# Start of a conformer/attention encoder kernel: two output pairs share the activations, squares summed in PSUM, first loads in halves on two queues, and a bias table written head by head in the weight queue

## The chip, the cores and the metric

The kernel runs on one core of a Trainium2 chip as one launch. The metric is the device time of that launch in microseconds. The kernel before takes 2254.43 us (median of 3 runs, 2253.42 to 2255.34). A core has a matrix engine (TensorE, PE in the profile; its weight loads are PEld), VectorE (DVE), ScalarE (ACT), GpSimd (POOL) and SyncE (SP), which here only issues DMAs. ACT and POOL issue DMAs as well. All engines run their own instruction streams in order and meet at semaphores.

## The reference

The input is x of shape 1 x 256 x 2048 in float32. Layer 0 is a conformer convolution module and a convolutional feed-forward network; layer 1 is differential attention and a second such network; each is added to x, with an RMS norm in front of it and one at the very end.

```
for i in range(2):
    h = rmsnorm(x, mix_norm[i])
    m = conformer_conv(h, ...) if i == 0 else diff_attention(h, ..., rel_bias, lambda_init)
    x = x + m
    x = x + conv_ffn(rmsnorm(x, ffn_norm[i]), ...)
return rmsnorm(x, final_norm_g)

conformer_conv: u = h @ w_in + b_in              # 2048 -> 4096
                a, gate = split(u);  u = a * sigmoid(gate)
                u = silu(layernorm(causal_dwconv31(u) + dw_b))
                return u @ w_out + b_out
diff_attention: 16 heads, two score maps each; bias_table[h, bucket(k - q)] is added
                to the scores and keys of later 64-chunks are masked
conv_ffn:       u = causal_dwconv3(h @ w_up);  (silu(gate) * val) @ w_down
```

## The kernel before

Everything is held transposed: channels in the 128 partitions, the 256 positions along the free axis. x is 8 tiles `X[pr]` of 128 x 2 x 256. A weight matrix is used in **pairs**: 2 x 128 output channels, for which the 16 input tiles of 128 channels are gone through in 4 **steps** of 4. Each step has its own weight tile of 128 x 1024 (512 KB). To keep float32 accuracy every operand is split into a rounded part `hi` and a remainder `lo`, and a product is three matmuls: hi by hi, hi by the activation's lo, lo by hi. A step of the module w_in is 24 such matmuls of 256 columns, a pair 96.

A weight tile comes through SP's queue into one of 5 `raw` buffers (`load_w`), ACT rounds it into one of 6 `hi` buffers and DVE or POOL subtracts to give one of 6 `lo` buffers (`split_w`; the argument `lo` of `pair` names the engine). `ahead` keeps the splits 4 steps in front of the matmuls and the loads 5 in front of the splits. An activation tile is split by one ACT and one DVE instruction (`split_act`, L279 and L280).

`setup` issues the first loads, splits 4 weight tiles and the 16 activation tiles in a hand-written order for DVE, ACT and POOL, squares x on ACT and sums the squares on DVE in SBUF (`x_square`, L326 to L333), and then computes the norm: `norm_cols` adds the halves and sums over channels with ones-matmuls (L286), raises the mean square to the power -1/2 on POOL (L298, `rc`), and `norm_rows` spreads the result over the partitions with two matmuls (L292) and copies it to `rstd`. The matmuls of w_in don't wait for the norm, since rstd is multiplied onto their result.

`conv_module` has 16 w_in pairs. After a pair, `post` multiplies the PSUM tile by rstd (L453), takes the sigmoid gate and writes `u` into a padded buffer `cpad` (L457). PSUM has two tiles `pp` for pairs, so pair 2 needs pair 0's post to be done. Then u is written to DRAM (`ud`, L469) and read back in four shifted copies (`R`, L473); POOL builds 32 x 32 diagonals `dg` from the filter (L482); `taps` runs 12 of the 31 filter taps as matmuls (L498), and DVE adds the other 19 (L536). After the first pair POOL also writes the 18 diagonals of the last pair (L489, `Y` and `A`). What is deferred by `at` runs so many steps later; elsewhere the order on an engine is set by the framework's scheduler.

`attn_setup` runs at the first step of layer 0's feed-forward network. It makes the 16 x 384 table of relative biases, writes it 128 times per head to DRAM as `d1` with one DMA from POOL (L759, 3 MB), and writes the mask into each head's part with 16 more (L766). In the attention `bias` reads a skewed 128 x 256 view of a head's part into `bm` (L851).

Of the kernel before, what the change touches and what calls it, by code (L numbers as in the profile page):

```python
# [61 lines left out]
class Builder:  # L62
# [72 lines left out]
    def load_w(self):  # L135
        i = self.np_
        self.np_ += 1
        w = self.W[i]
        w["raw"] = self.rawp.tile([P, self.c.NW], F32, tag="raw", name=self.nm("raw"))
        self.nc.sync.dma_start(w["raw"][:, :w["n"]], w["src"])  # L140

    def split_w(self):
# [7 lines left out]
        nc.scalar.copy(hi[:, :n], raw[:, :n])  # L150
        eng = nc.gpsimd if w["lo_eng"] == "g" else nc.vector
        ins = eng.tensor_tensor(lo[:, :n], raw[:, :n], hi[:, :n].bitcast(F32), ALU.subtract)  # L152
        if w["lo_eng"] == "g":
            self.pool_lo = ins.ins
        w["hi"] = hi[:, :n].rearrange("p (k c) -> p k c", c=w["cols"])
        w["lo"] = lo[:, :n].rearrange("p (k c) -> p k c", c=w["cols"])

    def ahead(self, i):

        N = len(self.W)  # L160
        while self.ns < min(N, i + 1):
# [158 lines left out]
    def x_square(self, st, pr, eng=None):  # L320
# [3 lines left out]
        if st["n"] == 0:  # L324
            st["ssq"] = self.const.tile([P, 2, S], F32, tag="ssq", name=self.nm("ssq"), bufs=1)
            nc.scalar.activation(st["ssq"], x, AF.Square)  # L326
        else:
# [4 lines left out]
            else:  # L332
                (eng or nc.gpsimd).tensor_tensor(st["ssq"], st["ssq"], sq, ALU.add)  # L333
        st["n"] += 1

    def norm_cols(self, st):
# [3 lines left out]
        self.nc.vector.tensor_tensor(f, q[:, 0, :], q[:, 1, :], ALU.add)  # L340
# [8 lines left out]
        self.rsqrt_cols(st["rc"], ps[:, 0:4:2], 1.0 / self.c.D)  # L349
# [41 lines left out]
    def setup(self, n0):  # L391
# [22 lines left out]
        with self.tc.manual_schedule(engines={ET.DVE, ET.Activation, ET.Pool}):  # L414
            for pr in range(KT // 2):
                if pr % 2 == 0 and pr // 2 < 4:
                    self.split_w()
                for j in range(2):
                    m = 2 * pr + j
                    n0["xh"][m] = self.act_tile()  # L420
                    self.split_act(n0["xh"][m][1], self.X[pr][:, j, :], self.col("mixg", m))

            for pr in range(KT // 2):
                if pr % 3 == 2:
                    self.ahead(4 + pr // 3)
                self.x_square(n0, pr, nc.vector)
        self.norm_cols(n0)
        self.norm_rows(n0)
# [6 lines left out]
        for i in range(3):  # L435
# [6 lines left out]
    def conv_module(self, nin, nout):  # L442
# [6 lines left out]
        def post(i, ps):  # L449
            with self.tc.high_priority():  # L450

                t = ps[:, :, 0:S]
                nc.vector.tensor_tensor(t, t, nin["rstd"].unsqueeze(1).to_broadcast([P, 2, S]), ALU.mult)  # L453
                sg = self.b1("G")
                nc.scalar.activation(sg, t[:, 1, :], AF.Sigmoid, bias=self.col("bin", KT + i))
                u = self.cpad[i % 3]
                nc.vector.scalar_tensor_tensor(u[:, CK - 1:CK - 1 + S], t[:, 0, :], self.col("bin", i), sg, ALU.add,  # L457
# [18 lines left out]
            queue = self.tc.issue_after(self.pool_lo) if i == 0 else ExitStack()  # L476
            with queue:
# [189 lines left out]
        for i in range(KT):  # L667
            off = self.pair(a["w_in"], off, c.kcs, lambda k: nin["xh"][k], lambda ps, i=i: post(i, ps),
# [406 lines left out]
```

## Time and profile before

| | before |
|---|---|
| median of 3 runs | 2254.43 us |
| profiled execution, its own time | 2254.46 us |
| span of its trace | 2252.7 us |
| PE busy | 2205.2 us (98%) |
| DVE busy | 1634.2 us (73%) |
| ACT busy | 1200.7 us (53%) |
| POOL busy | 273.5 us (12%) |
| DMA, mean over the span | 185 GB/s |
| mean granted TensorE clock | 0.991 |

The span runs from the first to the last instruction; the launch's own time is 1.8 us longer. A busy PE is not a PE at full pace: matmuls overlap and their ends are modelled. So stretches are compared by how many matmuls they hold, and gaps by the idle time that the timeline gives in brackets together with what ended it.

### The profile page before, as it was taken

The numbers are of one execution on the slowest core, as the hardware profiler recorded it, in microseconds if no ns is written. First come the engines' busy times: TensorE is split into PE (matmuls) and PEld (weight loads), VectorE is DVE, ScalarE is ACT, GpSimd is POOL, SyncE is SP. The second block draws the span as 40 slices with busy tenths as digits, with TensorE's granted clock in tenths as the row PEclk, the third lists the DMA queues.
The fourth block names the chain that finished last, engine by engine and source line by source line (L and its number), as shares of the span: only waits on it lengthen the run. The fifth ranks groups of instructions, "written<-read, shape, count | busy, mean of one in ns | idle before, by whom it ended". The sixth has DMA issues, their size and how long they took to land.

```text
span 2252.7 us, 34458 instructions
## 1 busy us (share of the span) xinstructions
PE 2205.2 (98%) x13238; PEld 1937.4 (86%) x13238; DVE 1634.2 (73%) x2471; ACT 1200.7 (53%) x1796; POOL 273.5 (12%) x181
## 2 busy tenths in 40 slices
PE   5999899999999999999999999999999999999998
PEld 5999788888888888888888888888888888888887
DVE  4788675877767777677777787767777677676774
ACT  4333454655545555455565665555555455554554
POOL 4788500100000000000100000100000000000002
PEclk8999999999999999999999999999999999999998
DMA  6677357866666666666655555566666666666662
GB/s 236 192 218 215 112 185 164 244 187 189 188 189 191 189 188 187 192 189 186 193 176 177 171 171 174 170 192 186 190 187 187 188 188 187 190 188 190 187 188 94
DMA packets 126004, 417.51 MB, mean 185 GB/s; under 512 B 14416, under 2 KB 26704, under 8 KB 125840
## 3 DMA queue, kind: packets, MB, share of 16 engines
q1 hardware_dynamic: 113040, 400.42, 57.2%
q10 hardware_dynamic: 11520, 11.45, 2.0%
q0 software_dynamic: 1280, 3.46, 1.3%
q8 instruction: 103, 1.69, 0.3%
q14 instruction: 61, 0.50, 0.1%
HBM read 407.55 MB, written 7.72 MB: 184 GB/s over the span
## 4 chain that ended last, share of the span: by engine, by line
PE 94%; DMA 2%; DVE 0%; issue 0%; ACT 0%; POOL 0%; ACTq 0%; POOLq 0%; DVEq 0%
PE pp L238 48%; PE pp L239 25%; PE pp L229 7%; PE pp L236 4%; PE pp L235 2%; PE pp L813 1%; PE pp L815 1%; PE pp L814 1%; DMA raw<-in_w_up_dram 1%; PE s L863 1%; PE s L498 1%; PE o L898 0%; DMA R<-ud 0%; PE t L498 0%; PE s L507 0%; DMA ud<-cpad 0%
## 5 line engine op out<-in xcount | busy, mean ns | idle before, releaser
L238 PE MATMUL pp<-act,hi 128*128 128x512 f32 x3902 | 1380.7, 396 | 5.8 <-DVE act L645 3.1
L239 PE MATMUL pp<-act,lo 128*128 128x256 f32 x3902 | 1095.7, 281 | 0.0
L150 ACT CAST hi<-raw 128x1024 fp32r<-128x1024 f32 x752 | 788.1, 1049 | 532.2 <-PE pp L238 186.2
L152 DVE TENSOR_TENSOR lo<-raw,hi 128x1024 fp32r<-128x1024 f32 x686 | 844.4, 1232 | 299.2 <-ACT hi L150 287.5
L238 PEld LDWEIGHTS pp<-act,hi 128*128 128x128 f32 x3902 | 732.5, 188 | 165.6 <-DVE act L645 3.4
L239 PEld LDWEIGHTS pp<-act,lo 128*128 128x128 f32 x3902 | 739.4, 189 | 10.2
L238 PE MATMUL pp<-actb,hi 128*128 128x512 f32 x856 | 308.5, 397 | 1.4 <-ACT hi L150 1.4
L239 PE MATMUL pp<-actb,lo 128*128 128x256 f32 x856 | 241.3, 282 | 0.8 <-DVE lo L152 0.8
L333 POOL TENSOR_TENSOR ssq<-ssq,Z 128x512 f32<-128x512 f32 x24 | 35.6, 1484 | 1518.4 <-ACT Z L329 1518.3
L229 PE MATMUL pp<-act,hi 128*128 128x256 f32 x1088 | 203.4, 289 | 9.0 <-ACT act L279 6.2
L238 PEld LDWEIGHTS pp<-actb,hi 128*128 128x128 f32 x856 | 161.3, 188 | 40.2 <-ACT hi L150 1.7
L229 PEld LDWEIGHTS pp<-act,hi 128*128 128x128 f32 x1088 | 173.7, 196 | 15.5 <-ACT act L279 6.2
L152 POOL TENSOR_TENSOR lo<-raw,hi 128x1024 fp32r<-128x1024 f32 x66 | 158.0, 2413 | 56.3 <-ACT hi L150 55.6
L239 PEld LDWEIGHTS pp<-actb,lo 128*128 128x128 f32 x856 | 162.6, 190 | 1.2 <-DVE lo L152 1.1
L266 ACT COPY E<-pp 128x512 f32<-128x512 f32 x104 | 60.9, 585 | 184.1 <-PE pp L236 184.1
L229 PE MATMUL pp<-act,lo 128*128 128x256 f32 x544 | 156.4, 288 | 2.0 <-POOL lo L152 1.5
L382 ACT COPY E<-pp 128x512 f32<-128x512 f32 x109 | 63.9, 586 | 170.7 <-PE pp L236 163.0
L268 DVE TENSOR_TENSOR E<-pp,E 128x512 f32<-128x512 f32 x104 | 71.9, 691 | 108.2 <-ACT E L266 108.2
L704 DVE SCALAR_TENSOR_TENSOR Y<-fpad,prm,Y 128x256 f32<-128x256 f32 x352 | 146.9, 478 | 0.0
L384 DVE TENSOR_TENSOR x<-pp,x 128x512 f32<-128x512 f32 x101 | 69.8, 691 | 87.8 <-ACT E L382 87.4
L701 ACT ACTIVATE Y<-fpad,prm 128x256 f32<-128x256 f32 x176 | 96.3, 595 | 48.3 <-DVE fpad L697 48.3
L229 PEld LDWEIGHTS pp<-act,lo 128*128 128x128 f32 x544 | 106.7, 196 | 2.4 <-POOL lo L152 1.7
(194 smaller groups left out, 1797.5 us busy)
## 6 DMA issues: line engine op xcount, KB each, us to landing
raw<-in_w_up_dram SPq DMA_DIRECT2D x352, 512.0 KB, 4.1
raw<-in_w_down_dram SPq DMA_DIRECT2D x176, 512.0 KB, 4.1
raw<-in_w_in_dram SPq DMA_DIRECT2D x64, 512.0 KB, 4.4
raw<-in_w_qk_dram SPq DMA_DIRECT2D x64, 512.0 KB, 3.6
raw<-in_w_out_dram SPq DMA_DIRECT2D x32, 512.0 KB, 3.8
raw<-in_w_v_dram SPq DMA_DIRECT2D x32, 512.0 KB, 3.7
raw<-in_w_o_dram SPq DMA_DIRECT2D x32, 512.0 KB, 3.8
R<-ud ACTq DMA_DIRECT2D x52, 132.0 KB, 4.8
```

What stands on the lines that cost most here:

```text
L150: nc.scalar.copy(hi[:, :n], raw[:, :n])
L152: ins = eng.tensor_tensor(lo[:, :n], raw[:, :n], hi[:, :n].bitcast(F32), ALU.subtract)
L229: nc.tensor.matmul(ps[:, 0:S], w[:, kk, cs], xt[:, x, :], start=(k == first and n == 0), stop=(k == last and n == 2))
L236: nc.tensor.matmul(*main, start=False, stop=True)
L238: nc.tensor.matmul(*main, start=(k == first), stop=False)
L239: nc.tensor.matmul(*corr, start=False, stop=False)
L266: nc.scalar.copy(cs, ps[:, :, S:])
L268: nc.vector.tensor_tensor(t, ps[:, :, 0:S], cs, ALU.add)
L382: nc.scalar.copy(cs, ps[:, :, S:])
L384: nc.vector.tensor_tensor(x, ps[:, :, 0:S], x, ALU.add)
L701: nc.scalar.activation(y[:, j, :], u[:, j, FK - 1:], AF.Identity, scale=self.col("fw", ch * FK + FK - 1), bias=self.col("fb", ch))
L704: nc.vector.scalar_tensor_tensor(y[:, j, :], u[:, j, q:q + S], self.col("fw", ch * FK + q), y[:, j, :], ALU.mult, ALU.add)
```

## The change

It has five parts. (1) The steps of w_in pairs 0 and 1 alternate, so each activation tile serves both before the next is needed; pair 2 writes into the PSUM tiles `s` and `t` instead of a pair tile, the posts of pairs 0 and 1 come two steps later, and there are 4 cpad buffers. (2) The `lo` parts of the first 12 weight tiles are made by DVE; POOL's first subtractions (tiles 12 to 16) are issued behind the norm's power, and the diagonals of the last pair are built in five portions, after pairs 1 to 5. (3) The sum of squares lies in PSUM, and its squares stand between the splits. (4) The first weight tile is loaded and split in halves; the first two x tiles are issued by ACT; 7 matmuls on a tile of ones run first. (5) The bias table goes to DRAM once (`tab`), and each head's 128 copies are written from there by SP, 16 + 8h steps later; the mask is set in SBUF by POOL after `bm` has landed.

```
 def load_w:
+        n = w["n"] // 2 if i == 0 else w["n"]
+        for o in range(0, w["n"], n):
+            self.nc.sync.dma_start(w["raw"][:, o:o + n], w["src"][:, o:o + n])
+            yield
 def split_w:
+        m = n // 2 if i == 0 else n
+        for o in range(0, n, m):
+            p = slice(o, o + m)
+            nc.scalar.copy(hi[:, p], raw[:, p])
+            with self.tc.issue_after(self.pow0) if w["lo_eng"] == "g" and 12 <= i < 17 else ExitStack():
+                ins = eng.tensor_tensor(lo[:, p], raw[:, p], hi[:, p].bitcast(F32), ALU.subtract)
 def x_square:
+            if st["first"]:
+                st["ssq"] = self.psx("s", [P, 2, S])
...
-                (eng or nc.gpsimd).tensor_tensor(st["ssq"], st["ssq"], sq, ALU.add)
+                (nc.vector if st["first"] else nc.gpsimd).tensor_tensor(st["ssq"], st["ssq"], sq, ALU.add)
 def setup:
+        warm = self.psx("t", [P, P])
+        for _ in range(7):
+            nc.tensor.matmul(warm, self.ones, self.ones, start=True, stop=True)
         for pr in range(KT // 2):
-            if pr % 2 == 0 and self.np_ < 4:
-                self.load_w()
-            nc.sync.dma_start(self.X[pr], a["x"][:, 2 * pr:2 * pr + 2, :])
+            if self.np_ < 5:
+                list(self.load_w())
+            (nc.scalar if pr < 2 else nc.sync).dma_start(self.X[pr], a["x"][:, 2 * pr:2 * pr + 2, :])
...
-        self.norm_cols(n0)
-        self.norm_rows(n0)
+        self.todo[7] = [lambda: self.norm_cols(n0)]
+        self.todo[8] = [lambda: self.norm_rows(n0)]
...
-        for i in range(3):
+        for i in range(4):
             t = self.ph1.tile([P, S + CK + 1], F32, name=f"cpad{i}", bufs=1)
 def conv_module:
-            queue = self.tc.issue_after(self.pool_lo) if i == 0 else ExitStack()
-            with queue:
+            with self.tc.issue_after(self.pool_lo) if i < 6 else ExitStack():
                 diagonals(i, g, dg)
...
-            if i == 0:
-                for j in range(0, c.ND, 4):
+            if 1 <= i <= 5:
+                for j in range(4 * (i - 1), min(4 * i, c.ND), 4):
...
-            off = self.pair(a["w_in"], off, c.kcs, lambda k: nin["xh"][k], lambda ps, i=i: post(i, ps),
-                            lo="v" if i == 0 else "vg" if i == 1 else "g", merged=True)
+            off = self.pair(a["w_in"], off, c.kcs, lambda k: nin["xh"][k],
+                            (lambda ps, i=i: self.at(2, lambda: post(i, ps))) if i < 2 else lambda ps, i=i: post(i, ps),
+                            lo="v" if i < 3 else "g", merged=True,
+                            halves=(lambda: [self.psx(b, [P, 512]) for b in "st"]) if i == 2 else None)
+            if i == 1:
+                self.interleave(0)
 def attn_setup:
+        tab = self.dr.tile([H, 384], F32, name="tab")
+        nc.gpsimd.dma_start(tab, tb)
         d1 = self.dr.tile([H, P, 384], F32, name="d1")
-        nc.gpsimd.dma_start(d1, tb.unsqueeze(1).to_broadcast([H, P, 384]))
...
-        mk = self.ph2.tile([64, 64], F32, name="mk")
-        nc.gpsimd.memset(mk, MASK)
+        def spread(h):
+            d = nc.sync.dma_start(d1[h], tab[h:h + 1, :].to_broadcast([P, 384]))
+            self.tc.keep_in_program_order(d)
         for h in range(H):
-            o = h * P * 384 + P - 1
-            nc.gpsimd.dma_start(self.bflat[o:o + 64 * 383].rearrange("(p d) -> p d", d=383)[:, S - 64:S], mk)
+            self.at(16 + 8 * h, lambda h=h: spread(h))
 def bias (attention):
+            nc.gpsimd.memset(BM[h][:64, S - 64:], MASK)
```

PE, from the last activation tile of pair 0's first pass: `pp_261` and `pp_399` are the PSUM tiles of pairs 0 and 1, `act_129` is the first activation tile and `act_186` the sixteenth. Before:

```order
L229 MATMUL pp_261<-act_186,hi_173 128x256 x2
L229 MATMUL pp_261<-act_186,lo_174 128x256
L229 MATMUL pp_399<-act_129,hi_204 128x256 x2
L229 MATMUL pp_399<-act_129,lo_205 128x256
L229 MATMUL pp_399<-act_129,hi_204 128x256 x2
L229 MATMUL pp_399<-act_129,lo_205 128x256
```

Now, at the fourth activation tile (`act_151`; the pairs are `pp_259` and `pp_284`, the first tile is `act_140`):

```order
L239 MATMUL pp_259<-act_151,hi_136 128x256 x2
L239 MATMUL pp_259<-act_151,lo_137 128x256
L239 MATMUL pp_284<-act_140,hi_156 128x256 x2
L239 MATMUL pp_284<-act_140,lo_157 128x256
L239 MATMUL pp_284<-act_140,hi_156 128x256 x2
L239 MATMUL pp_284<-act_140,lo_157 128x256
```

Pair 1's first step has moved from behind 16 activation tiles to behind 4.

PE, where the norm is spread over the partitions (L292 before, L302 now). Before it stands between pair 1 and pair 2 (`pp_533`):

```order
L229 MATMUL pp_399<-act_186,hi_342 128x256 x2
L229 MATMUL pp_399<-act_186,lo_343 128x256
L292 MATMUL o_243<-ident,rc_239 128x128 x2
L229 MATMUL pp_533<-act_129,hi_395 128x256 x2
L229 MATMUL pp_533<-act_129,lo_396 128x256
```

Now it stands in the last step of pair 2, whose two halves are `s_507` and `t_508`:

```order
L239 MATMUL s_507<-act_222,hi_461 128x256 x2
L239 MATMUL s_507<-act_222,lo_462 128x256
L239 MATMUL t_508<-act_222,hi_461 128x256
L302 MATMUL o_533<-ident,rc_497 128x128 x2
L239 MATMUL t_508<-act_222,hi_461 128x256
L239 MATMUL t_508<-act_222,lo_462 128x256
```

The matmuls that wait for `rc` have moved almost one pair back.

POOL, around the norm's power (`rc`). Before, behind the tables of the last pair (`A_391` is the end of them) and five weight tiles:

```order
L489 TENSOR_TENSOR A_391<-ident,cprm 128x256
L482 TENSOR_TENSOR dg_525<-cmask,cprm 128x384
L152 TENSOR_TENSOR lo_396<-raw_202,hi_395 128x1024
L152 TENSOR_TENSOR lo_427<-raw_217,hi_426 128x1024
L152 TENSOR_TENSOR lo_457<-raw_310,hi_456 128x1024
L152 TENSOR_TENSOR lo_487<-raw_340,hi_486 128x1024
L152 TENSOR_TENSOR lo_530<-raw_393,hi_529 128x1024
L298 TENSOR_TENSOR rc_239<-c_240,mhalf 128x2
```

Now it is POOL's first computation (`lo_504` is weight tile 12, the first of pair 3):

```order
L308 TENSOR_TENSOR rc_497<-c_498,mhalf 128x2
L163 TENSOR_TENSOR lo_504<-raw_369,hi_503 128x1024
L515 TENSOR_TENSOR dg_549<-cmask,cprm 128x384
L163 TENSOR_TENSOR lo_554<-raw_399,hi_553 128x1024
L515 TENSOR_TENSOR dg_592<-cmask,cprm 128x384
L522 TENSOR_TENSOR Y_594<-ident,cprm 128x512
L163 TENSOR_TENSOR lo_599<-raw_429,hi_598 128x1024
```

The weight tiles and the tables have moved from in front of the power to behind it.

## Rows read from the trace of the kernel before

**Rows 1.** Windows: span, busy per engine (instructions), granted clock, DMA share, GB/s

```profile
6.00:12.00 6.00, 5.18 (x23) 4.89 (x24) 5.09 (x10) 5.07 (x10) 0.00 (x0) 1.00 1.00 367
12.00:20.00 8.00, 8.00 (x69) 8.00 (x68) 6.45 (x13) 6.18 (x13) 0.00 (x0) 1.00 1.04 402
```

**Rows 2.** PE's timeline: start, length, what [idle before it, and what ended that]

```profile
35.00 0.61 PE L286 MATMUL o<-ones,M 128*128 128x2 f32 x4 [1.95 <-DVE M L346]
49.43 1.22 PE L292 MATMUL o<-ident,rc 128*128 128x128 f32 x4 [10.34 <-POOL rc L298]
52.87 0.80 PE L229 MATMUL pp<-act,hi 128*128 128x256 f32 x2 [2.22 <-DVE cpad L457]
61.35 1.50 PE L498 MATMUL s<-R,dg 128*32 128x256 f32 x24 [1.06 <-DMA R<-ud]
```

**Rows 3.** POOL's timeline before the norm's power

```profile
30.81 5.04 POOL L489 TENSOR_TENSOR Y<-ident,cprm 128x512 f32<-128x512 f32 x4
...
37.18 11.55 POOL L152 TENSOR_TENSOR lo<-raw,hi 128x1024 fp32r<-128x1024 f32 x5
48.69 0.69 POOL L298 TENSOR_TENSOR rc<-c,mhalf 128x2 f32<-128x2 f32 x1
```

**Rows 4.** DVE's timeline: the norm's mean square

```profile
35.65 0.16 DVE L297 TENSOR_SCALAR c<-o 128x2 f32<-128x2 f32 x1 [0.70 <-PE o L286]
```

**Rows 5.** Chain that ended last, 60 to 100 us: start, length, what

```profile
62.86 8.82 PE pp L229 x72
71.68 1.43 PE s L498 x24
...
86.67 11.71 PE pp L229 x96
```

**Rows 6.** Timeline, the first x loads and the first ACT work

```profile
1.17 0.90 SPq L407 DMA_DIRECT2D x<-in_x_dram  x2
...
2.47 0.20 ACT L401 ACTIVATE c<-ones 128x2 f32<-128x2 f32 x1
...
5.62 0.91 ACT L279 ACTIVATE act<-x,prm 128x256 fp32r<-128x256 f32 x2
```

**Rows 7.** Groups by form, 0 to 62 us: count | busy us, mean ns | idle before

```profile
L150 ACT CAST hi<-raw 128x1024 fp32r<-128x1024 f32 x16 | 16.4, 1044 | 21.3 <-DMA raw<-in_w_in_dram 13.4 <-DMA R<-ud 7.9
...
L279 ACT ACTIVATE act<-x,prm 128x256 fp32r<-128x256 f32 x16 | 7.0, 499 | 0.5 <-DMA x<-in_x_dram 0.5
...
L280 DVE SCALAR_TENSOR_TENSOR act<-x,prm,act 128x256 fp32r<-128x256 f32 x16 | 6.7, 479 | 0.0
...
L329 ACT ACTIVATE Z<-x 128x512 f32<-128x512 f32 x7 | 4.3, 626 | 2.4 <-DVE ssq L333 2.4
```

**Rows 8.** The page's costliest groups: DVE's weight remainder, whole span

```profile
L152 DVE TENSOR_TENSOR lo<-raw,hi 128x1024 fp32r<-128x1024 f32 x686 | 844.4, 1232 | 299.2 <-ACT hi L150 287.5
```

**Rows 9.** Groups by form, 64 to 225 us

```profile
L152 POOL TENSOR_TENSOR lo<-raw,hi 128x1024 fp32r<-128x1024 f32 x50 | 119.3, 2405 | 27.0 <-ACT hi L150 26.4 <-DMA raw<-in_w_in_dram 0.3 <-PE pp L229 0.2
...
L536 DVE SCALAR_TENSOR_TENSOR s<-cpad,cprm,s 128x256 f32<-128x256 f32 x164 | 79.6, 489 | 10.8 <-PE s L498 6.1
```

**Rows 10.** DMA issues, 366 to 412 us: count, KB each, median us to landing

```profile
raw<-in_w_up_dram SPq DMA_DIRECT2D x9, 512.0 KB, 22.5
d<-Z POOLq DMA_DIRECT2D x1, 3072.0 KB, 36.4
```

**Rows 11.** PE's timeline, 400 to 412 us

```profile
402.97 0.51 PE L238 MATMUL pp<-actb,hi 128*128 128x512 f32 x1 [1.40 <-ACT hi L150]
404.24 0.57 PE L239 MATMUL pp<-actb,lo 128*128 128x256 f32 x1 [0.76 <-DVE lo L152]
...
410.20 0.50 PE L238 MATMUL pp<-act,hi 128*128 128x512 f32 x1 [1.57 <-DVE E L268]
```

**Rows 12.** Windows, 404 to 408 us, columns as in rows 1

```profile
404.00:406.00 2.00, 1.76 (x6) 1.58 (x7) 1.00 (x3) 0.94 (x3) 0.66 (x2) 0.57 1.03 409
406.00:408.00 2.00, 2.00 (x9) 1.71 (x9) 0.36 (x1) 1.43 (x3) 2.00 (x4) 0.58 1.00 407
```

More of the change, by code (lines that the diff above doesn't have):

```diff
@@ L318, in x_done, with x_square @@
             self.x_square(st, pr)
[L320 removed]
+    def x_square(self, st, pr):
         nc = self.nc
@@ L339, in norm_cols @@
         f = self.b1("M")
-        self.nc.vector.tensor_tensor(f, q[:, 0, :], q[:, 1, :], ALU.add)
+        if st["first"]:
+            self.nc.scalar.copy(f, q[:, 0, :])
+            self.nc.vector.tensor_tensor(f, q[:, 1, :], f, ALU.add)
+        else:
+            self.nc.vector.tensor_tensor(f, q[:, 0, :], q[:, 1, :], ALU.add)
         srcs = [f]
@@ L414, in setup @@
         with self.tc.manual_schedule(engines={ET.DVE, ET.Activation, ET.Pool}):
[L415 to L426, printed above, removed]
-        self.norm_cols(n0)
-        self.norm_rows(n0)
+            for m in range(KT):
+                if m in (0, 2):
+                    first = self.split_w() if m == 0 else first
+                    next(first)
+                elif m % 4 == 0 and m < 12:
+                    self.ahead(self.ns)
+                n0["xh"][m] = self.act_tile()
+                self.split_act(n0["xh"][m][1], self.X[m // 2][:, m % 2, :], self.col("mixg", m))
+                if m % 4 == 3 and m < 12:
+                    self.ahead(self.ns)
+                if m % 4 == 3 and m > 4:
+                    for pr in (m // 2 - 3, m // 2 - 2):
+                        self.x_square(n0, pr)
+            for pr in (KT // 2 - 2, KT // 2 - 1):
+                self.x_square(n0, pr)
+        self.todo[7] = [lambda: self.norm_cols(n0)]
+        self.todo[8] = [lambda: self.norm_rows(n0)]
         self.fpad = []
@@ L450, in post @@
             with self.tc.high_priority():
-                t = ps[:, :, 0:S]
-                nc.vector.tensor_tensor(t, t, nin["rstd"].unsqueeze(1).to_broadcast([P, 2, S]), ALU.mult)
+                if isinstance(ps, list):
+                    t = [b[:, 0:S] for b in ps]
+                    for x in (1, 0):
+                        nc.vector.tensor_tensor(t[x], t[x], nin["rstd"], ALU.mult)
+                else:
+                    t = [ps[:, x, 0:S] for x in range(2)]
+                    nc.vector.tensor_tensor(ps[:, :, 0:S], ps[:, :, 0:S],
+                                            nin["rstd"].unsqueeze(1).to_broadcast([P, 2, S]), ALU.mult)
                 sg = self.b1("G")
-                nc.scalar.activation(sg, t[:, 1, :], AF.Sigmoid, bias=self.col("bin", KT + i))
-                u = self.cpad[i % 3]
-                nc.vector.scalar_tensor_tensor(u[:, CK - 1:CK - 1 + S], t[:, 0, :], self.col("bin", i), sg, ALU.add,
+                nc.scalar.activation(sg, t[1], AF.Sigmoid, bias=self.col("bin", KT + i))
+                u = self.cpad[i % 4]
+                nc.vector.scalar_tensor_tensor(u[:, CK - 1:CK - 1 + S], t[0], self.col("bin", i), sg, ALU.add,
                                                ALU.mult)
@@ L965, in encoder @@
     KT = cfg.KT
-    n0 = b.new_norm("mixg", 0)
+    n0 = b.new_norm("mixg", 0, first=True)
     n1 = b.new_norm("ffng", 0)
```

27 lines of the change are left out of this document (14 added, 13 removed).

## The prediction

> **What bounds the kernel now.** Read the page first: PE is busy for 98% of the span, so there is little to win in the bulk, and the question is where the other 2% and the slow stretches lie. Second, the windows: from 6 to 12 us PE holds 23 matmuls in 5.2 us, from 12 to 20 us 69 in 8.0 us [rows 1], so its first 5 us run at half pace. Third, PE's timeline, for gaps with a releaser: 1.95 us on the sum of squares, 10.34 us on the norm's power, 2.22 us on the first post and 1.06 us on the tap data, all before 61.4 us [rows 2]. Fourth, the queue behind the longest: the mean square is ready at 35.8 us [rows 4], but the power starts at 48.69 us, since POOL first builds the last pair's diagonals and then subtracts five weight tiles, 11.55 us [rows 3]. Fifth, the chain afterwards: one pair is 96 matmuls in 11.71 us with nothing between them [rows 5], a step therefore 2.93 us, and from 61.35 us PE does not wait any more in this module until its end.
>
> So the start can be accounted for. At 61.35 us PE has done pairs 0 and 1 and a quarter of pair 2 (72 of its 96 matmuls still follow [rows 5]): 2.25 x 11.71 = 26.3 us, and 1.8 us of norm matmuls [rows 2]. The remaining 33.2 us are lost. That is the pot for parts 1 to 4.
>
> The second place is the start of layer 0's feed-forward network. The bias DMA takes 36.4 us, and nine weight loads beside it have a median of 22.5 us to landing [rows 10]. PE waits 1.40 + 0.76 + 1.57 = 3.7 us [rows 11], and between 404.2 and 407.8 us it runs at a granted clock of 0.57 to 0.58 [rows 12], that is at 1.2 GHz for nearly all of it; half of some 3.5 us is another 1.8. Together 5.5 us.
>
> **Parts 1 to 4, step by step.** I date the first matmul of pair 3 in the new order, and compare it with the same point before: 71.68 us, the end of pair 2 [rows 5], less the 1.43 us of pair 0's taps, which now come later: 70.25 us.
>
> First block (4 activation tiles, both pairs). The first x tile was issued by SP at 1.17 us; on ACT it now stands behind the activation that ends at 2.67 us, 1.5 us later [rows 6]. ACT's first work on x began at 5.62 us without waiting for x [rows 6], so x had landed by then and now lands by 7.1 us at the latest. Then follow four activations of 0.50, half a rounding and a whole one of 1.04 [rows 7], 3.6 us, a remainder on DVE of 1.23 [rows 8], and pair 1's step on PE of nearly 2.9: the block ends by 14.7 us. Without any delay of x it would end at 13.2. I take 14.0, the middle; both ends go into the range.
>
> Here a rule speaks against the second queue. The Trainium skill (DMA: Bandwidth & Descriptors, section "Issuing engines are not separate DMA queues") says that DMAs of all issuing engines run on the same 16 engines and interleave, and that issuing from several saves only issue time. The share of 1.00 to 1.04 from 6 to 20 us [rows 1] agrees that the engines are full. By the rule the halves and the second queue bring no bytes earlier, and only the 1.5 us of delay are left: a block end of 14.7.
>
> Blocks 2 to 4 are 6 steps of 2.93, 17.6 us. Does the supply keep up? Per block of 5.86 us ACT has two roundings, four activations and two squares, 2 x 1.04 + 4 x 0.50 + 2 x 0.63 = 5.3 us [rows 7]; DVE two remainders and four splits, 2 x 1.23 + 4 x 0.48 = 4.4 us [rows 7, 8], which leaves 1.4 us for its two additions of squares. A block needs two weight tiles of 512 KB and two x tiles of 256 KB, 1.57 MB, which is 3.9 us at the 402 GB/s of rows 1. It just fits. POOL does nothing here, so no remainder waits for it. I allow 1.0 us in block 4, where the roundings stand behind activations and squares: eight steps are done at 32.6 us. Pair 2 takes 11.7 and the norm's matmuls about 1.5: 45.8 us. The power itself no longer waits: it needs 0.69 us on an empty POOL [rows 3], and PE has about a step and a half of pair 2 (some 3.4 us) between the channel sums and the rows. Were that cover gone, its price would be bounded by the 10.34 us of before; I take 0.
>
> Then a wait that is new in place: pair 3 needs pair 0's PSUM tile, whose post stands on DVE behind the two products of pair 2, which end with PE's last matmul. Before, the same post cost 2.22 us [rows 2]; a part now precedes, I take 1.4 (bounds 0.9 to 2.2). Pair 3 starts at 47.2 us. **Gain: 70.25 - 47.2 = 23.0 us.**
>
> What is late next? Three posts come together. Before, pair 0's u was ready at 52.87 us and its taps began at 61.35, 8.5 us later [rows 2]; now three of them share ACT's queue, and PE reaches the taps of pair 0 3.5 steps, 10.4 us, after the start of pair 3. Behind that, pair 3's taps need the accumulator of pair 0, whose 19 DVE taps now alternate with pair 1's: 38 x 0.489 [rows 9] and two posts, some 20 us from 11.8 us on, against PE's arrival after 9.4 steps and three tap groups, 31.8 us. Both have about no slack. I take 1.5 us lost for the two (bounds 0 and 6). POOL has 4 x 2.405 us per pair [rows 9] and at most two tables of 1.26 [rows 3], 12.1 us against PE's 11.71 + 1.43 = 13.1: it keeps up, with a lead of a step.
>
> The seven warming matmuls cost nothing while PE waits for data. The half pace of rows 1 came with PE's first 23 matmuls and ended about 12 us; if it stays as it was, block 1, half starved anyway, ends about 1 us later, which the range has. The Trainium skill (TensorE: Matmul & The Clock Gate, Part 1) says that the array starts and, after idling, returns to 1.2 GHz, and that matmuls warm it: by the rule the burst helps only if the gap to the first real matmul is short. The trace differs in one point: it lists a granted clock of 1.00 in both windows of rows 1, though the pace doubles between them. The sum stays as it is.
>
> **Part 5.** Each head's copy is 192 KB. At the rate of before, 3072 KB in 36.4 us [rows 10], one takes 2.3 us, and there is one in every 8 steps, some 23 us, in front of weight loads that are issued 5 tiles ahead. That hides it; the 5.5 us come back. Bounds: 3.7 if a clock dip stays, 0 if the copies still hold the loads up. The 16 small fills on POOL are bounded by 0 and 16 x 0.7 = 11 us (the smallest POOL operation in rows 3, none hidden); bm is loaded at the start of its head's pair and read two steps after the pair's end, and POOL otherwise has one power per head there, so 0.
>
> **Sum.** 23.0 - 1.5 + 5.5 = 27.0 us. The profiled execution took 2254.46 us, 1.8 more than its span and within 0.1 of the median of 2254.43. So 2254.46 - 27.0 = **2227.5 us**.
>
> **Rivals.** (A) The front fills worse: the block supply runs at its limit on ACT and DVE, and the R chain comes late by half of its 8.5 us. Then 3 us more in the blocks and 4 at the taps: 2234.5. For it: supply figures of 5.3 and 5.8 against 5.86, and no slack at the taps. Against: those are means with overlap not taken off. (B) It fills better: x lands early, the tap waits vanish, block 4 has none: 1.5 + 0.8 + 1.0 less, and PE's first gaps shrink: 2223. (C) The bias copies only move their stall: 5.5 us are not won, 2233. Against it: 192 KB at a time with pauses. (D) Slower than before: reading one 1.5 KB row 128 times from DRAM could be far slower than reading it from SBUF, as before. A weight load has about 5 steps, 14 us, before it is missed; a copy that holds the queue for longer stalls PE by the excess, 16 times. From 14 + 27/16 = 15.7 us per copy (7 times the 2.3 us of rows 10) the whole gain is gone; at 20 us it is 16 x 6 = 96 us, 2323. (E) The change doesn't do what it says: the order of the new kernel shows the interleaved pairs and the power in front of POOL's work, so a wait of the old size there is all but excluded.
>
> **How the numbers follow.** Main case 0.6 (2223 to 2232), A 0.2, B 0.08, C 0.07, D 0.03, the rest for smaller gains. The range 2218 to 2241 holds the main case, A, B and C with a reserve. About 0.2%, 4.5 us, is what a measurement of this kernel tells from no change: faster by more 0.95, within 0.02, slower 0.03.
>
> **What would show it.** Right: the longest PE gap in the first 60 us is under 3 us; the power starts within 1 us of the mean square; pair 3's first matmul is near 47 us and pairs then follow at 13.1 us; no granted clock under 0.9 near 380 us, and weight loads landing evenly beside the 16 copies. Wrong: gaps at the rounding or remainder in every block (A), PE waiting for R or for DVE's accumulator for over 4 us (A), a dip every 8 steps in the feed-forward network (C, D), or gaps in the attention that end with a fill on POOL.

## The result, and the profile after

Over the executions compared on one chip the median went from 2254.89 us to 2228.82 us (2227.41 to 2233.2 in four), a ratio of 0.9887 with a 95% interval of 0.9870 to 0.9904. Predicted were 2227.5 us, 2218 to 2241. The profiled execution is the longest of the four, 2233.2 us, of which 2231.4 are its span; its mean granted clock is 0.993, the three others have 0.994 to 0.996.

The answers to [rows 2] first. PE's timeline at the same points of the program: the norm's channel sums (L296) and rows (L302), pair 3's first matmul, and the taps whose wait a releaser is named for.

```profile
39.65 0.50 PE L296 MATMUL o<-ones,M 128*128 128x2 f32 x4
43.45 0.60 PE L302 MATMUL o<-ident,rc 128*128 128x128 f32 x4
46.89 0.51 PE L239 MATMUL pp<-act,hi 128*128 128x256 f32 x2 [1.16 <-DVE cpad L491]
59.31 1.50 PE L531 MATMUL s<-R,dg 128*32 128x256 f32 x24 [1.96 <-DMA R<-ud]
63.33 1.50 PE L531 MATMUL s<-R,dg 128*32 128x256 f32 x24 [1.13 <-DMA R<-ud]
...
83.66 1.50 PE L531 MATMUL s<-R,dg 128*32 128x256 f32 x24 [1.43 <-DMA R<-ud]
```

The 1.95 and 10.34 us in front of sums and rows are gone, the post's 2.22 became 1.16, and the one wait for tap data of 1.06 became three, 4.5 us together. Pair 3 starts at 46.89 us. DVE's mean square and POOL's power, the answers to [rows 3, 4], now stand 0.24 us apart (13.0 before):

```profile
40.19 0.16 DVE L307 TENSOR_SCALAR c<-o 128x2 f32<-128x2 f32 x1 [4.13 <-PE o L296]
```
```profile
40.43 0.70 POOL L308 TENSOR_TENSOR rc<-c,mhalf 128x2 f32<-128x2 f32 x1 [39.99 <-DVE c L307]
41.09 2.41 POOL L163 TENSOR_TENSOR lo<-raw,hi 128x1024 fp32r<-128x1024 f32 x1
```

The windows of [rows 1], and 8 to 10 us apart (stretch, length, PE, PEld, DVE, ACT, POOL busy, granted clock, DMA share, GB/s):

```profile
6.00:12.00 6.00, 5.29 (x25) 4.56 (x26) 4.17 (x7) 4.41 (x8) 0.00 (x0) 0.63 1.00 385
8.00:10.00 2.00, 1.43 (x5) 0.90 (x5) 0.89 (x2) 1.65 (x3) 0.00 (x0) 0.50 1.01 398
12.00:20.00 8.00, 8.00 (x60) 8.00 (x60) 6.79 (x13) 5.86 (x11) 0.00 (x0) 0.85 1.05 396
```

The start is no faster than before: 25 matmuls by 12 us (23 before), then 60 in 8 us (69). Here the clock is listed as 0.50, and it stays there until 14.4 us.

At the feed-forward network's start the windows of [rows 12] and the DMA issues of [rows 10] answer (count, KB each, median us to landing):

```profile
400.00:412.00 12.00, 12.00 (x71) 10.49 (x70) 8.36 (x12) 6.79 (x10) 0.00 (x0) 1.00 0.65 203
404.00:406.00 2.00, 2.00 (x13) 1.77 (x12) 2.00 (x5) 1.05 (x3) 0.00 (x0) 1.00 0.65 172
406.00:408.00 2.00, 2.00 (x13) 1.77 (x12) 1.66 (x3) 1.26 (x2) 0.00 (x0) 1.00 0.51 137
```
```profile
raw<-in_w_up_dram SPq DMA_DIRECT2D x17, 512.0 KB, 3.6
d<-tab SPq DMA_DIRECT2D x2, 192.0 KB, 4.2
```

PE never stops, at full clock, and loads land in 3.6 us instead of 22.5.

### The profile page after: what moved, and what is told of

Its sections match the earlier page's. It is cut to its first block, busy times and chain, and to the rows that moved or that the text cites. A ratio compares the mean times of both kernels' runs of the same rounds, so it can differ in the third digit from the quotient of the medians.

```text
span 2231.4 us, 34500 instructions
## 1 busy us (share of the span) xinstructions
PE 2203.6 (99%) x13252; PEld 1936.9 (87%) x13252; DVE 1624.9 (73%) x2481; ACT 1201.4 (54%) x1798; POOL 250.8 (11%) x174
## 4 chain that ended last, share of the span: by engine, by line
PE 95%; issue 2%; DMA 1%; POOL 1%; DVE 0%; ACT 0%; POOLq 0%; ACTq 0%; DVEq 0%
PE pp L248 49%; PE pp L249 25%; PE pp L239 6%; PE pp L246 4%; PE pp L245 2%; PE pp L854 1%; PE pp L856 1%; PE pp L855 1%; DMA R<-ud 1%; PE s L906 1%; PE s L531 1%; PE o L941 0%; PE s L540 0%; PE t L531 0%; PE s L248 0%
## 5 line engine op out<-in xcount | busy, mean ns | idle before, releaser
L160 ACT CAST hi<-raw 128x1024 fp32r<-128x1024 f32 (+1 forms) x753 | 788.4, 1048 | 511.5 <-PE pp L248 190.4
L163 DVE TENSOR_TENSOR lo<-raw,hi 128x1024 fp32r<-128x1024 f32 (+1 forms) x693 | 850.0, 1228 | 287.7 <-ACT hi L160 286.2
L248 PEld LDWEIGHTS pp<-act,hi 128*128 128x128 f32 x3902 | 732.4, 188 | 163.9 <-DVE act L678 3.4
L249 PEld LDWEIGHTS pp<-act,lo 128*128 128x128 f32 x3902 | 738.3, 189 | 10.3
L239 PE MATMUL pp<-act,hi 128*128 128x256 f32 x1024 | 189.5, 287 | 3.5 <-ACT act L289 2.2
L239 PEld LDWEIGHTS pp<-act,hi 128*128 128x128 f32 x1024 | 161.6, 194 | 9.7 <-issue 4.9
L163 POOL TENSOR_TENSOR lo<-raw,hi 128x1024 fp32r<-128x1024 f32 x60 | 142.7, 2401 | 21.1 <-ACT hi L160 14.5
L569 DVE SCALAR_TENSOR_TENSOR s<-cpad,cprm,s 128x256 f32<-128x256 f32 x182 | 85.3, 486 | 24.0 <-PE s L531 20.4
```

What stands on the lines that cost most here:

```text
L160: nc.scalar.copy(hi[:, p], raw[:, p])
L163: ins = eng.tensor_tensor(lo[:, p], raw[:, p], hi[:, p].bitcast(F32), ALU.subtract)
L239: nc.tensor.matmul(ps[:, 0:S], w[:, kk, cs], xt[:, x, :], start=(k == first and n == 0), stop=(k == last and n == 2))
L248: nc.tensor.matmul(*main, start=(k == first), stop=False)
L249: nc.tensor.matmul(*corr, start=False, stop=False)
L569: nc.vector.scalar_tensor_tensor(acc, u[:, j:j + S], self.col("cw", i * CK + j), acc, ALU.mult, ALU.add)
```

## The experiments

Every ratio is to the kernel before, in executions on the same chip; the intervals are 0.0012 to 0.0017 wide to either side, some 3 us. So the large steps are resolved, and steps of 1 to 2 us are read from traces and called unresolved in time. "Pair 3", "R" and "w_out" are from the one profiled execution: pair 3's first matmul, PE's waits for tap data up to w_out, and w_out's first matmul.

| run | median us | ratio [95%] | pair 3 | R | w_out |
|---|---|---|---|---|---|
| before | 2254.89 | 1 | 67.3 (derived) | 1.1 + 0.5 | 263.23 |
| changed | 2228.82 | 0.9887 [0.9870, 0.9904] | 46.89 | 4.5 | 248.31 |
| e0 the same again | 2229.01 | 0.9891 [0.9877, 0.9904] | 47.00 | 3.0 | 245.88 |
| e1 bias part alone | 2247.07 | 0.9968 [0.9956, 0.9981] | | 0.9 + 0.5 | 263.41 |
| e2 taps later | 2227.23 | 0.9881 [0.9868, 0.9895] | 46.19 | 0.6 | 243.15 |
| e3 pair 3's lo on DVE | 2232.34 | 0.9901 [0.9886, 0.9916] | 50.22 | 0 | 249.48 |
| e4 no alternation | 2232.42 | 0.9903 [0.9889, 0.9916] | 48.03 | 3.3 | 250.12 |
| e5 no warming | 2229.99 | 0.9892 [0.9879, 0.9906] | 45.88 | 3.2 | 246.38 |
| e6 x on SP | 2228.99 | 0.9887 [0.9872, 0.9902] | 47.25 | 3.0 | 246.15 |
| e7 POOL's order of before | 2241.12 | 0.9940 [0.9927, 0.9952] | 53.94 | 3.1 | 255.67 |
| e8 squares in SBUF | 2230.18 | 0.9899 [0.9883, 0.9916] | 47.25 | 2.0 | 246.57 |
| e9 taps later, 5 buffers | 2227.80 | 0.9884 [0.9869, 0.9898] | 45.58 | 0 | 241.34 |
| e10 fill at the layer norm | 2227.98 | 0.9887 [0.9872, 0.9902] | 45.53 | 2.5 | 243.04 |
| e11 e9 and e10 | 2226.14 | 0.9873 [0.9856, 0.9889] | 45.45 | 0.2 | 241.68 |

**e0.** No edit.

> The changed kernel once more, with another profile. Theory: its median is 2227 to 2229 us, 0.988 to 0.989 of before, and what set the profiled execution of the first result (2233.2 us) apart from the other three (2227.4 to 2230) is a longer stretch at the half clock in the first 15 us, so that the mean granted clock (0.993 there, 0.994 to 0.996 in the others) goes with the time, about 2.2 us for each 0.001. Rival: the spread has nothing to do with the clock, and the times do not follow it. In either case pair 3 starts at 46 to 48 us and PE waits for R about 4 to 5 us in three places.

The level is confirmed, and the times follow the clock (0.993: 2230.7 and 2233.2 in the two profiled executions; 0.995 to 0.996: 2227.4 to 2229.1), by 0.7 (e0) and 1.9 us (changed) for each 0.001 from 0.993 to 0.996, less than the 2.2 expected. But the first 15 us are not what set the first profile apart: the half pace ends at 14.4 us there and at 14.6 in e0, and pair 3 starts within 0.11 us. The two profiles draw apart by 1.5 us at R, which is late in two places here and not in three, and by another 1.0 up to w_out.

**e1: part 5 alone.** The kernel before with this edit:

```
-        nc.gpsimd.dma_start(d1, tb.unsqueeze(1).to_broadcast([H, P, 384]))
+        nc.gpsimd.dma_start(tab, tb)
...
+            d = nc.sync.dma_start(d1[h], tab[h:h + 1, :].to_broadcast([P, 384]))
+            self.at(16 + 8 * h, lambda h=h: spread(h))
...
+            nc.gpsimd.memset(BM[h][:64, S - 64:], MASK)
```

> The kernel before with the bias table written by head in the weight queue, and nothing else of the change. Theory: it gives back the 3.7 us of waits and 1.8 us of half clock at the start of layer 0's feed-forward network, up to the 6.4 us by which the two profiles draw apart behind the first module: 2248.4 to 2249.5 us, and its trace has no wait of PE between 400 and 412 us. Rival: the difference behind the first module is mostly chance or the clock, and this part alone gives under 2 us (over 2252.5). Other rival: the copies cost some of it again elsewhere, and the gain is under 4 us.

7.1 us, somewhat over the theory, which lies inside the interval; both rivals fall. The window from 400 to 412 us, before and then in e1, holds 36 and 71 matmuls: 35 missing ones at 5.9 per us are 5.9 us.

```profile
400.00:412.00 12.00, 8.28 (x36) 6.44 (x35) 6.37 (x10) 7.23 (x12) 5.52 (x11) 0.86 0.96 301
400.00:412.00 12.00, 12.00 (x71) 10.49 (x70) 9.49 (x15) 6.70 (x10) 0.00 (x0) 1.00 0.67 204
```

The other parts are worth the rest, e0 against e1 on one chip: 2247.07 - 2229.01 = 18.1 us.

**e7: POOL's order.** Remainders, tables and diagonals on POOL as before, nothing held behind the power:

```
-            with self.tc.issue_after(self.pow0) if w["lo_eng"] == "g" and 12 <= i < 17 else ExitStack():
+            with ExitStack():
...
-            with self.tc.issue_after(self.pool_lo) if i < 6 else ExitStack():
+            with self.tc.issue_after(self.pool_lo) if i == 0 else ExitStack():
...
-            if 1 <= i <= 5:
+            if i == 0:
...
-                            lo="v" if i < 3 else "g", merged=True,
+                            lo="v" if i == 0 else "vg" if i == 1 else "g", merged=True,
```

> The changed kernel with POOL's work as it was: remainders of pairs 1 and 2 on POOL again, in part, the tables all behind pair 0's diagonals, and nothing held behind the norm's power, which then stands behind seven remainders, two sets of diagonals and five tables. Theory: this order is what made the power late before (10.34 us of PE's wait), and it decides most of the gain of the start: the power comes 5 us or more behind the sums, PE waits for it 4 to 10 us in front of pair 3, and the time is 2233 to 2239 us. Rival: the work that the alternation gives PE (pairs 0 to 2 all before the power) covers it whatever POOL does, and the time stays within 2 us of 2229; R may even come earlier, since the weight loads are no longer held behind the power.

12.1 us of the 18.1 go with this edit alone; the theory named the place, but the price is past its range. (Between the profiled executions of e7 and e0 it is 8.5 us: e7's is the fastest of its five, e0's the slowest of its four.) POOL's timeline shows the queue in front of the power, which comes 12.3 us after the mean square at 36.80, and PE's shows what followed:

```profile
25.47 15.24 POOL L163 TENSOR_TENSOR lo<-raw,hi 128x1024 fp32r<-128x1024 f32 x6 [8.81 <-ACT hi L160]
40.67 0.83 POOL L515 TENSOR_TENSOR dg<-cmask,cprm 128x384 f32<-128x384 f32 x1
41.46 4.05 POOL L522 TENSOR_TENSOR Y<-ident,cprm 128x512 f32<-128x512 f32 x4
...
49.13 0.70 POOL L308 TENSOR_TENSOR rc<-c,mhalf 128x2 f32<-128x2 f32 x1
```
```profile
49.88 1.22 PE L302 MATMUL o<-ident,rc 128*128 128x128 f32 x4 [5.81 <-POOL rc L308]
53.94 0.79 PE L239 MATMUL pp<-act,hi 128*128 128x256 f32 x2 [2.84 <-DVE cpad L491]
```

The waits are 5.81 and 1.7 more at the post, 7.5 us. The rows take 1.22 us where they took 0.60: the clock is at 0.50 after the wait, and stays there up to 58 us, so pair 3's first 4 us ran at half pace, another 2 us. These 9.5 us are what the trace accounts for; the rest of the 12.1 is not located. The kernel before had the same behind its 10.34 us, which the prediction did not mention. Two windows of before:

```profile
48.00:50.00 2.00, 0.57 (x2) 0.57 (x3) 0.00 (x0) 0.00 (x0) 2.00 (x3) 0.50 0.75 233
54.00:56.00 2.00, 2.00 (x11) 2.00 (x11) 0.00 (x0) 0.00 (x0) 0.00 (x0) 0.50 0.73 254
```

**e4: no alternation.**

```
-            if i == 1:
-                self.interleave(0)
```
(and the post of pair 0 five steps after its last step instead of two, so that it stays behind the norm's rows)

> The changed kernel without the alternation: the steps of pair 0 and then of pair 1, everything else of the change as it is (the post of pair 0 stays behind the norm's rows). Theory: the alternation is what lets ACT put the squares between the activations, since a block of two steps, 5.9 us of PE, then covers 5.3 us of ACT. Without it pair 0's four steps need all 16 activations by 23 us, and ACT has some 4.2 us of work per step of 2.93 us: PE waits 3 to 5 us in pair 0, pair 3 starts at 50 to 52 us, and the time is 2232 to 2234 us. Rival: in the kernel before, pair 0 came first as well and PE hardly waited in it from 8 to 32 us; then the alternation is worth under 1.5 us (2227.5 to 2230), and the whole gain of the start is the earlier power and the cover for it.

2232.42 us lies in the theory's range, but not by its mechanism: pair 3 starts at 48.03 us and not at 50 to 52, and PE's waits for activation tiles in the first 60 us are 3.1 us (e0: 2.2), not 3 to 5 more. Part of the difference is the clock, which stood at 0.50 until 18.1 us in this profile (14.6 in e0) and again from 59.0 to 62.4, behind the wait of 3.28 us for R. Among executions with a mean clock of 0.995 or 0.996 it has 2231.0 and 2231.2, e6 on the same chip 2227.9 to 2230.5: the alternation is worth some 2 us, at the edge of what can be told.

**e3: pair 3's remainders on DVE.**

```
-                            lo="v" if i < 3 else "g", merged=True,
+                            lo="v" if i < 4 else "g", merged=True,
```
(and the first diagonals, which then have no remainder on POOL ahead of them, are not held)

> The changed kernel with the remainders of pair 3's weights on DVE and not on POOL, where they stood behind the norm's power. Theory: R is late because the weight buffers of pair 3 stay occupied until the power is done (41 us), DMA idles from 38 to 44 us, and the held loads then run beside the R copies. With the remainders on DVE the loads go on, R lands earlier, and 2 to 4.5 us of the R waits go: 2223.5 to 2226.5 us. Rival: DVE has no room there (4 x 1.23 us more ahead of pair 0's post), the post comes later, PE's wait before pair 3 grows from 1.2 to 3 us or more, R is later still, and the time is 2228 to 2233 us.

Both were half right: the time and the longer wait are the rival's, but PE does not wait for R any more. Windows of e0 and then of e3 show the held loads as described (DMA share 0.00 to 0.04 against 0.93 to 1.01); in e3 the loads stand still later, at 46 to 50 us:

```profile
38.00:40.00 2.00, 2.00 (x19) 2.00 (x19) 0.00 (x0) 0.84 (x1) 0.00 (x0) 1.00 0.04 14
40.00:42.00 2.00, 2.00 (x19) 2.00 (x19) 0.16 (x1) 0.21 (x1) 1.46 (x2) 1.00 0.00 0
```
```profile
38.00:40.00 2.00, 2.00 (x19) 2.00 (x19) 1.56 (x2) 0.41 (x2) 0.00 (x0) 1.00 0.93 338
40.00:42.00 2.00, 2.00 (x19) 2.00 (x18) 1.06 (x1) 0.91 (x1) 0.00 (x0) 1.00 1.01 414
...
46.00:48.00 2.00, 0.81 (x5) 0.52 (x4) 0.18 (x1) 1.42 (x2) 2.00 (x2) 1.00 0.00 0
...
50.00:52.00 2.00, 1.78 (x8) 1.79 (x9) 0.94 (x3) 0.32 (x1) 1.24 (x1) 0.50 0.81 299
54.00:56.00 2.00, 2.00 (x11) 2.00 (x11) 0.00 (x0) 0.00 (x0) 0.00 (x0) 0.50 1.06 313
```

Part of R's gain may be that PE itself came later: it reached pair 0's taps at 59.80 us, where e0 began to wait for them at 57.44. PE idles before pair 3:

```profile
45.13 0.50 PE L296 MATMUL o<-ones,M 128*128 128x2 f32 x4
46.67 0.71 PE L302 MATMUL o<-ident,rc 128*128 128x128 f32 x4 [0.57 <-POOL rc L308]
50.22 0.80 PE L239 MATMUL pp<-act,hi 128*128 128x256 f32 x2 [2.84 <-DVE cpad L491]
```

DVE ends the sum of squares at 42.5 us instead of 36.2, with two of the remainders in between, and PE's order has the channel sums behind 285 of the 288 matmuls of pairs 0 to 2 instead of behind 246, so that hardly any work is left to cover the power and the post. After 0.57 and 2.84 us of waits the clock fell to 0.50 and came back near 56 us: another 3 us of work lost. The idle of 1.16 us in the changed kernel cost no clock.

**e2 and e9: taps later.** Asked for two steps later; e9 has a fifth u buffer as well. (In e2 one of pair 0's 19 taps on DVE reads u after pair 4 has overwritten it; the instructions are the same.)

```
-            self.at(5 if i < KT - 2 else 4, lambda: taps(i, u, R, dg))
+            self.at(7 if i < 4 else 5 if i < KT - 2 else 4, lambda: taps(i, u, R, dg))
```

> The changed kernel with the taps of pairs 0 to 3 two steps later on PE. Theory: PE's 4.5 us of waits for R vanish, as R lands by 83.4 us at the latest for the last of them, and the time falls to 2223 to 2225 us. Rival: the wait moves on, since everything behind the taps (DVE's 19 taps in the accumulators, their layer norm) is also 5.9 us later: PE then waits for an accumulator or a PSUM tile by pair 3's taps or at the layer norm's barrier, and the time stays within 1.5 us of 2228.

> The changed kernel with the taps of pairs 0 to 3 asked for two steps later and a fifth buffer for u, so that no pair's u is overwritten before its taps have read it. On PE the four groups then stand at steps 16.1, 17.0, 19.4 and 23.0 instead of 15.5, 16.0, 19.4 and 21.4. Theory: R's waits of 3.0 to 4.5 us fall under 1 us and nothing takes their place, as in the run with four buffers (2227.23): 2224.5 to 2227.5 us. Rival: behind pair 3 the taps of pair 4 follow after only two steps, and their R, or DVE's accumulators, are late instead: the time is within 1 us of 2229.

R's waits fall to 0.6 and 0, and w_out starts 2.7 and 4.5 us before e0, of which 0.8 and 1.4 were there at pair 3 already. Nothing takes the waits' place. The medians move by 1.2 to 1.8 us, the right way and unresolved; both miss the theory's range, e2 by 2.2 us and e9 by 0.3.

**e5, e6, e8: the small parts undone.** No warming matmuls; all x on SP; the first sum of squares in SBUF and without the copy.

```
-        warm = self.psx("t", [P, P])
-        for _ in range(7):
-            nc.tensor.matmul(warm, self.ones, self.ones, start=True, stop=True)
```
```
-            (nc.scalar if pr < 2 else nc.sync).dma_start(self.X[pr], a["x"][:, 2 * pr:2 * pr + 2, :])
+            nc.sync.dma_start(self.X[pr], a["x"][:, 2 * pr:2 * pr + 2, :])
```
```
-            if st["first"]:
-                st["ssq"] = self.psx("s", [P, 2, S])
...
```

> The changed kernel without the seven warming matmuls. Theory: they do nothing for the half pace, since it lasted to 14 us with them (2 us windows of the first profile: clock 0.50 from 8 to 14 us) and to 12 us in the kernel before without them: 2227.5 to 2230.5 us, and the stretch of half pace after PE's first real matmul is as long as with them, 6 to 9 us. Rival: without them the half pace lasts longer, and the time is 2 to 4 us more (2231 to 2233). Other rival: the count for the return to full clock starts with PE's first real matmul instead of the first warming one, 5 us later, and the half pace lasts to 17 us or more.

> The changed kernel with all x tiles on SP's queue, in the order of the program (first weight tile in halves, first x tile, and so on). Theory: the second queue brings no bytes earlier, and x is no longer behind the first activation on ACT; but on SP the second x tile stands behind the second weight tile of 512 KB, so the block's third and fourth activation come later by about 1.3 us of DMA. The first matmul comes 0 to 1 us earlier, the first block ends within 1 us of before, and the time is 2227.5 to 2230 us. Rival: the two queues do share the load better, and without the second one x comes 2 to 3 us later: 2230.5 to 2232 us.

> The changed kernel with the first norm's sum of squares in SBUF, as before, and without the copy on ACT that the PSUM sum needs at its end. Theory: where the sum lies decides nothing, since PE has steps of pairs 1 and 2 to do until the channel sums and does not wait for them in the changed kernel: pair 3 still starts at 46 to 48 us, and the time is 2227.5 to 2230.5 us. Rival: DVE's adds from SBUF take longer or collide with POOL, DVE falls behind in its remainders, PE waits in the blocks, and the time is 2231 or more.

None can be told from the changed kernel, and no rival is borne out. By the pace of the matmuls, the half pace ended at 11.4 us without the warming; with it, it ended at 14.4 and 14.6 us (changed, e0), 12.4 (e2), 10.8 (e10) and 9.7 (e11), which are the same kernel up to there: it varies from execution to execution, and the seven matmuls do not set it. With x on SP the second wait for ACT grows from 0.55 to 1.38 us, and the first shrinks by 0.13. Pair 3 starts 0.25 us later in e6 and in e8.

**e10 and e11: fill at the layer norm.** Matmuls of the ones tile, results unread, in PE's three waits behind pair 15, each group issued after the last matmul ahead of it; e11 has e9's edit too.

```
+    def fill(self, out, n):
+        with self.tc.issue_after(self.last):
+            for _ in range(n):
+                self.nc.tensor.matmul(out, self.ones, self.ones, start=True, stop=True)
...
+                        self.fill(box["ps"][:, 0, 0:P], 8)
...
+                self.fill(ps[:, 8:], 5)
...
+            self.fill(rp[0][:, 0:P], 4)
```

> The changed kernel with matmuls of the ones tile, whose results nobody reads, in PE's three waits at the layer norm behind pair 15: five before the last channel sums (wait of 2.6 us), four before the norm's rows (1.5 us), eight before the first step of w_out (3.1 us). Theory: in the second profile of the changed kernel the granted clock fell to 0.50 at 240.0 us, 4.4 us after the first of these waits began, and came back at 250.1; in it the rows took 2.07 us where the first norm's four took 0.60, and w_out's first 4.2 us went at half pace. If PE's own idling is what lowers the clock, as the 3.4 us of waits before pair 3 in the run with DVE's remainders suggest (0.50 from 50 to 56 us), the fill keeps it at 1.00, and 1.0 + 2.1 us come back: 2225.5 to 2227.5 us. Rival: the clock falls whatever PE does with such small matmuls (they did not help at the start), the fill itself runs at half pace, eight take 4.8 us instead of the 3.1 they lie in, and the time is 2229 to 2231 us.

> The changed kernel with both edits that helped in the traces: the taps of pairs 0 to 3 later with a fifth u buffer, and the matmuls of the ones tile in PE's three waits at the layer norm. Theory: the two lie in different places, one before 84 us and one from 232 us, so they add: R's waits of 3.0 us go, and the barrier and w_out's first steps give 2 to 3 us (10.1 us instead of 11.3 from the sums to the first step, no half pace behind it). Alone they moved the median by about 1 us each, less than the traces promise; together 2223 to 2226.5 us, faster than both kernels, and 0.986 to 0.988 of before. Rival: what each wins in its profile is lost elsewhere in other executions (a half pace at the start that lasts longer or shorter by several us), and the median stays within 1 us of 2228.

PE's timeline there, e0 and then e10:

```profile
238.17 0.58 PE L296 MATMUL o<-ones,act 128*128 128x2 f32 x4 [2.61 <-DVE act L602]
...
240.72 2.07 PE L302 MATMUL s<-ident,c 128*128 128x128 f32 x8 [1.53 <-POOL c L649]
245.88 0.80 PE L248 MATMUL pp<-act,hi 128*128 128x512 f32 x1 [3.09 <-DVE act L678]
```
```profile
236.12 0.61 PE L303 MATMUL o<-ones,act 128*128 128x2 f32 x4 [0.60 <-DVE act L609]
...
237.04 1.14 PE L179 MATMUL s<-ones 128*128 128x128 f32 x8
238.71 1.16 PE L309 MATMUL s<-ident,c 128*128 128x128 f32 x8 [0.54 <-POOL c L659]
239.71 1.95 PE L179 MATMUL pp<-ones 128*128 128x128 f32 x16
243.04 0.50 PE L253 MATMUL pp<-act,hi 128*128 128x512 f32 x1 [1.38 <-DVE act L689]
```

In e10 the clock stays at 1.00 throughout, the rows take 1.16 us instead of 2.07, and the first matmul of w_out 0.50 instead of 0.80. In e11 it still fell, but only from about 235.0 to 238.4 us (e0: 239.9 to 250.2), and w_out started at full clock:

```profile
234.00:236.00 2.00, 2.00 (x13) 2.00 (x14) 0.48 (x3) 0.40 (x1) 0.18 (x1) 0.74 0.00 0
236.00:238.00 2.00, 2.00 (x11) 2.00 (x10) 0.37 (x3) 0.00 (x0) 0.54 (x1) 0.50 0.00 0
238.00:240.00 2.00, 2.00 (x19) 2.00 (x18) 1.45 (x4) 0.45 (x2) 0.08 (x1) 0.90 0.01 4
```

In all twelve traces without fill the clock fell to 0.50 at this layer norm, for 10.2 to 13.7 us; with fill it did not, or for 3.4 us. So PE's idling here brings the clock down, and fill shortens or prevents that. In e11 w_out starts no earlier than in e9 (241.68 and 241.34 us); the gain lies behind: from w_out's first matmul to the last input tile of its first pair PE takes 21.2 us in e10 and e11, 22.9 in e0 and 23.0 in e9. In time e10 alone is unresolved, and its median misses the theory's range by 0.5 us. e11, 2225.17 to 2227.02 us, lies wholly under the changed kernel's 2227.41 to 2233.2 and under e0's 2228.7 to 2230.73, though the intervals of the ratios overlap: its median of 2226.14 us, inside the theory's range, is the lowest of the study, 2.7 us under the changed kernel's. From e9's 2225.3 to 2228.61 it cannot be told.

## Why the prediction was right, and where not

The time was right to 1.3 us, and the mechanism: a power freed from POOL's queue, its wait covered by PE's own work, and a stall removed at the feed-forward network. e1 and e7 show the stall and POOL's order as the two large pieces, 7.1 us and 12.1 of 18.1. The cover, with pair 2 in `s` and `t` and the norm's rows at its end, stands in every one of these kernels but e1 and was not priced alone. That the number came out so near is in part luck: two terms of the sum were too favourable (by 2.6 and by 1.5 to 3.0 us), one was too small (by 0.4 to 1.6), and on the way to pair 3 the errors cancel.

**Pair 3's start: right; what it was compared with: wrong.** Forecast 47.2 us with 1.4 of wait, measured 46.89 with 1.16. But the way there was another. Counted in PE's timeline, the first block's 48 matmuls end at 16.05 us, 2 us behind the forecast 14.0 and past the late bound of 14.7, because the half pace lasted to 14.4 (in e10, where it ended at 10.8, they end at 14.7). Blocks 2 to 4 take 17.3 us without a gap, so the 1.0 us allowed in block 4 was not needed, and pair 2 with the norm's matmuls takes 12.4 us instead of 13.2. These errors offset each other. The step that failed is "71.68 us, the end of pair 2". In the order of the kernel before, 240 matmuls of w_in stand ahead of pair 0's taps and 312 ahead of the next. A pair has 96, so at 61.35 us PE had done 2.5 pairs and not 2.25, and the 72 matmuls of [rows 5] reach one step into pair 3. The reference is 71.68 - 1.43 - 2.93 = 67.3 us, and the gain there 20.4 us, not 23.0.

**The taps: 3.0 to 4.5 us, not 1.5** (bounds 0 and 6). PE waits for R, whose queue on ACT and whose copies the prediction did name; it did not see that the remainders held behind the power keep weight buffers occupied, so that DMA stands still from 38 to 44 us and the late loads then run beside R's copies: from 36 to 86 us these land in a median of 6.5 us (5.9 in e0), in e3 in 5.0. e3, where the loads go on from 38 to 44 us, agrees with that, but since PE also came to the taps later there, how much of R's wait is due to it is not shown. The feared wait for DVE's accumulators did not come.

**Part 5: 7.1 us, not 5.5.** By matmuls missing from 400 to 412 us it is 5.9; from 377 us, where before and e1 stand within 0.1 us of each other, to the last norm's sums they draw apart by 6.2 us. Another 1.1 us arise behind, where the last rows ran at 0.50 in the profile of before and at 1.00 in e1's (1.23 and 0.71 us for the first four); nothing shows that part 5 has to do with that. A copy lands in 4.2 us against 2.3 estimated, far from the 15.7 at which it would have cost; fills on POOL cost nothing seen.

With the measured terms: 20.4 - 4.5 + (5.9 to 7.1) is 21.8 to 23.0 us for the profiled execution, which won 21.3. e0's profile, with 20.3 and 3.0, gives 23.2 to 24.4, against 23.7. Both are the slowest executions of their four, and both won less than the 27.0 us forecast. The medians, 2228.82 and 2254.89 us, are 26.1 us apart. e10's profile, whose edit begins behind 230 us, is one more sample of the start: pair 3 at 45.53 us and 2.5 us for R give 21.8 - 2.5 + (5.9 to 7.1), 25.2 to 26.4.

**The rivals.** A's place was right for the taps, 3 to 4.5 us where it asked for 4, and the 4.5 us of the first profile are past the 4 us that the prediction called a sign of A; of its late blocks only the first was late, mainly by the clock. B's early x did not come, C and D fell with e1, E with the power's row. The rule of the Trainium skill (DMA: Bandwidth & Descriptors, "Issuing engines are not separate DMA queues"), that issuing from several engines saves only issue time, is agreed with by e6 within the 3 us that the medians resolve: x on one queue or two gives 2228.99 and 2229.01 us. That the warming matmuls cost and bring nothing is agreed with by e5.

What stays open: why the clock's half pace at the start ends anywhere from 9.7 to 18.1 us (half of that spread, some 4 us, is an estimate of what it can move a single execution by), how much of e4's 3.4 us is the alternation, and what the cover alone is worth.

## What to carry to other kernels

Date a common point of two programs by counting instructions in their order, not by reading which block a row seems to belong to: here that was 2.9 us of the 23. A short operation on a slow engine's queue is worth moving ahead of bulk work, but what is held behind it keeps buffers, and these keep loads. An idle of TensorE is paid twice when its clock falls: look at the granted clock behind each wait of some us, and at independent work that could lie in it.

## What the runs showed of the hardware

Waits of 10.34 us (before), 5.81 + 2.84 (e7), 0.57 + 2.84 (e3) and 2.6 + 1.5 + 3.1 (layer norm) went with a granted clock of 0.50, that is 1.2 GHz, for 6 us or more; a wait of 1.16 us did not. In between the length of the wait does not decide: 1.95 us on the sums (before) and 3.28 us on R (e4) were followed by 0.50, from 35.6 to 39.1 and from 59.0 to 62.4 us, while 2.04 us (e0) and 3.15 us (e7), both on R, were not. Near the start every trace has a stretch of half pace, either from the first matmuls of w_in on (before, e1, e2, e3, e5, e7, e9, e11) or after some three to ten at full pace (the changed kernel, e0, e4, e6, e8, e10), in most of them behind 3.3 us of warming ones. The listed clock can be wrong there: in e3 it reads 1.00 from 8 to 14 us while a group of two 128x256 matmuls takes 0.63 us, which takes 0.40 later.
